# One fixed order for the chunks of eight MoE experts, two norm rows loaded earlier, and the first splits on GpSimd moved

## The chip, the core and the metric

The kernel runs on one core of a Trainium2 chip, as one launch. The core has a matrix engine (TensorE, here PE), a vector engine (VectorE, DVE), a scalar engine (ScalarE, ACT), GpSimd (POOL) and SyncE (SP), which here issues most of the loads. They run side by side and wait for each other by semaphores. The metric is the device time of one execution in microseconds (us); lower is better. All data are float32; a wide product is written as three matmuls of rounded high parts (H) and rests (L) of its factors.

## The reference

The network is two layers of a first block and then one layer of a second block, on 256 positions of width 1024. The change touches the second layer's mixture of experts (MoE), and the norms that stand between the stages. Cut to that:

```python
def swiglu(x, w1, w3, w2):
    return (jax.nn.silu(x @ w1) * (x @ w3)) @ w2

def moe_swiglu(x, router_w, w1, w3, w2):
    logits = (t @ router_w).astype(jnp.float32)      # t: 256 x 1024, 8 experts
    top_v, top_i = lax.top_k(logits, 2)
    gates = jax.nn.softmax(top_v, axis=-1)
    combine = jnp.sum(one_hot(top_i, 8) * gates[..., None], axis=1)
    for e in range(8):
        out = out + combine[:, e:e + 1] * swiglu(t, w1[e], w3[e], w2[e])   # 1024 -> 3584 -> 1024

x = layer_norm(ALPHA * x + mixer(x), ln1_g, ln1_b)
x = layer_norm(ALPHA * x + ffn_or_moe(x), ln2_g, ln2_b)   # dense FFN in layer 0, MoE in layer 1
# block 2: h = rms_norm(x, norm1_g); ... h = rms_norm(x, norm2_g); conv FFN; final norm
```

## The kernel before

**Stages.** Layer 0 (mixer, dense FFN), layer 1 (mixer, MoE), block 2 (mixer, FFN) run one behind the other. The MoE takes from about 660 to 1632 us of the trace.

**Experts and parts.** The router ranks seven of the experts by how many positions they got; expert 0 stands apart. Each rank has slots for a fixed number of positions. Expert 0 and ranks 1, 2, 3 are *wide* (128 slots); ranks 4 to 7 are *narrow* (64 slots). Rank 1 has a narrow part of 64 more slots on the same weights; its chunks are called *heavy* here. If a rank has more positions than slots, a branch (`If`, L1392) runs a second pass; in these runs it isn't taken.

**Chunks.** An expert's 3584 hidden columns are 7 chunks of 512. A chunk needs three loads of 2 MB (`raw`, issued by SP at L155): two up matrices and one down matrix; the down matrix is loaded behind the next chunk's up matrices, since a chunk's down product runs one step later. There are six `raw` buffers, taken in turn. A wide chunk splits its weights (L170 the cast to H on ACT, L172 the subtraction to L on DVE, 12 of each per chunk) and does 48 matmuls up and 24 down in threes (`mm3`, L176 to L178). A narrow part uses the float32 weights as they are, on 64-column halves of the array (`side`, L1247): 64 matmul records up and 16 down, and nothing on ACT and DVE for the weights. So a narrow chunk brings as many bytes as a wide one with less matmul work, and a heavy chunk is a wide and a narrow one's matmuls on one chunk's bytes.

**Gather and scatter.** `gather` (L1144) picks an expert's positions by products with a one-hot matrix `oh` (L1173); the results go to `g` (wide) and `gx` (narrow). `scatter` (L1190) turns `oh`, scales the accumulators `acc` by the gates (L1219, L1220), multiplies by the turned `oh` (L1230) and adds to the stream `xn` (L1231).

**The order of the work.** `moe` (L1357) hands `experts` four groups: (expert 0, rank 4), (rank 2, rank 5), (rank 1 with its second part, rank 7), (rank 3, rank 6). In a group wide and narrow chunks alternate one to one (`turns`; the first group's `lead` begins with two wide ones). A group has one gather and one scatter for all its parts. What else sets the order is the scheduler of the framework, which puts each engine's instructions in a row.

**Norm rows and held splits.** Behind the MoE a layer norm and an RMS norm run for each half (128 positions) of `xn`. The layer norm's g row is loaded into the buffer `rscr`, which the last scatter uses before, ahead of the branch; the b row into `yL` behind the branch (both by ACT's queue, L276). `finish` sets a list `hold` for the first four splits of the next stage: two on GpSimd, issued after the instruction `p`, two on DVE, issued after the last rest of the transposed `xn`. In before, `p` is GpSimd's own power (`rsqrt`, L188) of the second half's norm. `finish` is called at four places that matter: behind layer 0's mixer (about 211 to 224 us), the dense FFN (411 to 424), the MoE (1637 to 1656), and block 2's mixer (1767 to 1781).

## Time and profile before

| | us |
|---|---|
| three runs | 2001.13, 2006.73, 2010.96 |
| median | 2006.73 |
| the profiled execution's own time | 2001.22 |
| its span, first to last instruction | 1999.4 |
| MoE, from the first narrow silu (698.08) to the last (1614.37) | 916.3 |

In the profile, PE is the share of the span in which matmuls run, PEclk the granted clock of TensorE as a part of its full speed, DMA share the mean busy share of the core's 16 DMA engines. "Idle before <-releaser" names what ended an engine's last wait. In a timeline, instructions of one line that follow each other are one row with their count. The PE is busy for 91% of the span, DVE for 60%, ACT for 42%, POOL for 10%; DMA moves 242 GB/s on average. A silu (L1316 wide, L1321 narrow) ends a chunk's up product and is a good clock of the chunks.

### The profile page before, as it was taken

The page shows a single profiled execution, that of the slowest core. Times are in us where ns is not written, and L with a number is a line of the kernel's source. Part 1 is how long each engine was busy: PE and PEld are TensorE (multiplying, and loading weights), DVE is VectorE, ACT ScalarE, POOL GpSimd, SP SyncE. Part 2 cuts the span into 40 slices and gives each one's busy share as a digit, 9 for nine tenths or more (in the row PEclk, how much of TensorE's full clock was granted, in tenths as well). Part 3 has the DMA queues.
Part 4 walks back from the last instruction along what each step waited for, and adds up shares of the span by engine and source line. Part 5 has one row for each costly group of instructions (what it writes and reads, how often), then busy time and mean ns, then how long its engine had stood idle before and what let it go on. Part 6 is the DMA issues. An engine that isn't in the chain of part 4 may idle for free. (4 is left out here: it accounts for less than half of the span.)

```text
span 1999.4 us, 28155 instructions
## 1 busy us (share of the span) xinstructions
PE 1819.5 (91%) x11670; PEld 1408.2 (70%) x11670; DVE 1197.6 (60%) x1717; ACT 842.3 (42%) x1176; POOL 203.4 (10%) x128
## 2 busy tenths in 40 slices
PE   7778899986878999998989999999999868989998
PEld 6666899975656766666666666666666637779997
DVE  6796654578785755355454544344553647667776
ACT  3234344433243545334343443343443525545554
POOL 4251200043323000000000000000000004010000
PEclk9788999998788999999999999999999988799999
DMA  6320536352204799999999777787999944134551
GB/s 241 118 94 23 190 137 243 127 215 85 95 13 169 282 430 418 388 393 355 363 393 384 300 297 305 307 342 315 365 414 390 399 156 164 43 135 171 185 195 64
DMA packets 37574, 484.76 MB, mean 242 GB/s; under 512 B 4544, under 2 KB 5184, under 8 KB 8000
## 3 DMA queue, kind: packets, MB, share of 16 engines
q1 hardware_dynamic: 34992, 475.74, 60.8%
q10 hardware_dynamic: 2448, 7.17, 1.1%
q8 instruction: 93, 1.52, 0.3%
q14 instruction: 41, 0.34, 0.0%
HBM read 481.84 MB, written 1.05 MB: 242 GB/s over the span
## 5 line engine op out<-in xcount | busy, mean ns | idle before, releaser
L172 DVE TENSOR_TENSOR wL<-raw,wH 128x1024 fp32r<-128x1024 f32 (+1 forms) x510 | 616.3, 1229 | 261.9 <-ACT wH L170 250.7
L170 ACT CAST wH<-raw 128x1024 fp32r<-128x1024 f32 x560 | 577.5, 1051 | 401.7 <-PE mm L177 154.0
L1247 PE MATMUL mm<-raw,gx 128*64 128x256 f32 x2240 | 252.3, 381 | 0.0
L1247 PEld LDWEIGHTS mm<-raw,gx 128*64 128x64 f32 x2240 | 156.6, 137 | 85.6 <-issue 10.8
L176 PE MATMUL acc<-wH,hH 128*128 128x512 f32 x408 | 163.8, 416 | 19.8 <-ACT wH L170 19.0
L176 PE MATMUL mm<-wH,g 128*128 128x512 f32 x448 | 177.1, 395 | 0.0
L177 PE MATMUL acc<-wL,hH 128*128 128x512 f32 x408 | 169.7, 416 | 7.2 <-DVE wL L172 7.1
L177 PE MATMUL mm<-wL,g 128*128 128x512 f32 x448 | 175.1, 391 | 0.0
L178 PE MATMUL mm<-wH,g 128*128 128x512 f32 x448 | 174.8, 390 | 0.0
L178 PE MATMUL acc<-wH,hL 128*128 128x512 f32 x408 | 166.8, 410 | 0.0
L172 POOL TENSOR_TENSOR wL<-raw,wH 128x1024 fp32r<-128x1024 f32 x50 | 126.1, 2532 | 135.2 <-ACT wH L170 122.3
L188 POOL TENSOR_TENSOR sm_brs<-sm_brs,half_neg 128x1 f32<-128x1 f32 x8 | 12.1, 1518 | 1207.2 <-DVE sm_brs L186 1207.2
L1247 PE MATMUL acc<-raw,hN 128*64 128x512 f32 x560 | 127.5, 597 | 0.0
L1321 ACT ACTIVATE ff<-mm 128x256 f32<-128x256 f32 x35 | 13.5, 385 | 247.8 <-PE mm L1247 247.8
L176 PEld LDWEIGHTS acc<-wH,hH 128*128 128x128 f32 x408 | 79.1, 197 | 44.4 <-ACT wH L170 22.5
L177 PE MATMUL mm<-b2yL,wH 128*128 128x256 f32 x384 | 109.7, 286 | 0.0
L176 PE MATMUL mm<-b2yH,wH 128*128 128x256 f32 x384 | 109.6, 286 | 0.0
L178 PE MATMUL mm<-b2yH,wL 128*128 128x256 f32 x384 | 109.4, 285 | 0.0
L1322 DVE TENSOR_TENSOR ff<-ff,mm 128x256 f32<-128x256 f32 x35 | 14.7, 421 | 157.2 <-ACT ff L1321 157.2
L177 PEld LDWEIGHTS acc<-wL,hH 128*128 128x128 f32 x408 | 80.2, 197 | 32.3 <-DVE wL L172 14.7
L176 PE MATMUL mm<-y0H,wH 128*128 128x256 f32 x352 | 100.1, 285 | 0.0
L178 PE MATMUL mm<-y0H,wL 128*128 128x256 f32 x352 | 99.8, 284 | 0.0
(518 smaller groups left out, 3263.2 us busy)
## 6 DMA issues: line engine op xcount, KB each, us to landing
raw<-in_moe_dram SPq DMA_DIRECT2D x168, 2048.0 KB, 9.7
raw<-in_ffn_dram SPq DMA_DIRECT2D x33, 2048.0 KB, 7.7
raw<-in_w_in_dram SPq DMA_DIRECT2D x13, 2048.0 KB, 9.2
raw<-in_w_o_dram SPq DMA_DIRECT2D x4, 2048.0 KB, 7.5
row<-in_ln_dram ACTq DMA_DIRECT2D x8, 512.0 KB, 3.6
raw<-in_w_out_dram SPq DMA_DIRECT2D x2, 2048.0 KB, 8.4
raw<-in_w_in_dram SPq DMA_DIRECT2D x3, 1024.0 KB, 5.1
raw<-in_ffn_dram SPq DMA_DIRECT2D x3, 1024.0 KB, 5.2
```

The costliest lines, as they stand in the source:

```text
L170: self.A.copy(H, src)
L172: (eng or self.V).tensor_tensor(L, src, H.bitcast(F32), OP.subtract)
L176: self.T.matmul(out, lhsT=lh, rhs=rh, start=start, stop=False)
L177: self.T.matmul(out, lhsT=lh, rhs=rl, start=False, stop=False)
L178: return self.T.matmul(out, lhsT=ll, rhs=rh, start=False, stop=stop)
L188: return self.G.tensor_tensor(out, out, self.half_neg.to_broadcast([P, n]), OP.pow)
L1247: T.matmul(out[i * 64:i * 64 + 64], lhsT=lhsT, rhs=rhs[:, i * n:i * n + n], start=start, stop=stop)
L1321: A.activation(sn[-1], b[:, 0:256], AF.Silu)
L1322: V.tensor_tensor(sn[-1], sn[-1], b[:, 256:512], OP.mult)
```

## The change

- **One list of steps.** The groups go. Four wide jobs run in the order expert 0, rank 2, rank 1 (heavy), rank 3. A table `FOLLOW` says how many narrow chunks (ranks 4, 5, 6, 7 in this order, 28 in all) follow each wide chunk: 3 in the first job, 4 in the second, 17 in the heavy one, 4 in the last.
- **A gather and a scatter for each job**, and so one for each of nine parts; `gx` has four 64-slot places in turn, and four accumulators are fixed for the whole MoE.
- **Norm rows.** The g and b row of the layer norm behind the MoE go into one tile `gb` of their own, loaded ahead of the branch.
- **Hold.** `layer_norm` and `rms` hand back their last DVE instruction, and `finish` gets that as `p`.

```diff
+FOLLOW = ((0, 1, 0, 1, 0, 1, 0), (1, 0, 1, 0, 1, 0, 1), (2, 3, 2, 3, 2, 3, 2), (1, 0, 1, 0, 1, 0, 1))
...
-        p = self.rsqrt(rs, mv[:, 1:2], 1.0, LN_EPS)
+        self.rsqrt(rs, mv[:, 1:2], 1.0, LN_EPS)
...
-        return p
+        return last
...
-        turns = [(j, c) for c in range(7) for j in range(2)]
...
-        lead = [(0, 0), (0, 1)] + [x for c in range(5) for x in ((1, c), (0, c + 2))] + [(1, 5), (1, 6)]
...
+        jobs = [(part(0), [(0, 0, 0)]), (part(2), [(0, 2, 0)]), (part(1), [(0, 1, 0), (1, 1, P)]), (part(3), [(0, 3, 0)])]
+        narrow = [(j, c) for j in range(4, 8) for c in range(7)]
+        jobs += [(part(r), [(2, r, 0)]) for r in range(4, 8)]
+
+        steps = []
+        for j, follow in enumerate(FOLLOW):
+            for c, n in enumerate(follow):
+                steps += [(j, c)] + narrow[0:n]
+                narrow = narrow[n:]
...
-        g = self.row(a["ln"][1, 2], "rscr")
+        gb = self.xp.tile([P, 2, D], F32, tag="xTL", name="gb", bufs=1)
+        for i in range(2):
+            A.dma_start(gb[:, i], a["ln"][1, 2 + i].partition_broadcast(P))
...
-        b, g2 = self.row(a["ln"][1, 3], "yL"), self.row(a["rows2"][0], "yH")
+        g2 = self.row(a["rows2"][0], "yH")
...
-            self.layer_norm(xn, t, g, b)
+            self.layer_norm(xn, t, gb[:, 0], gb[:, 1])
         for t in range(2):
-            p, *_ = self.rms(xn, t, g2, h)
+            *_, p = self.rms(xn, t, g2, h)
```

**TensorE, in the heavy expert.** `mm3` and `side` write `mm` for up products and `acc` for down products; `gx` holds narrow positions, `hN` a narrow part's hidden columns, `cst` is the identity of a transposition. Before, from a heavy chunk's last up matmul on:

```order
L178 MATMUL mm_9302<-wH_9390,g_8610 128x512
L1247 MATMUL mm_9303<-raw_9297,gx_8611 64x256 x16
L1247 MATMUL acc_9177<-raw_9299,hN_9293 64x512 x8
L182 MATMUL mm_9430<-cst_4_126,ff_9416 128x128 x4
L182 MATMUL mm_9439<-cst_4_126,ff_9419 128x128 x2
L1247 MATMUL mm_9450<-raw_9444,gx_8611 64x256 x16
L1247 MATMUL mm_9450<-raw_9446,gx_8611 64x256 x16
L176 MATMUL acc_8994<-wH_9486,hH_9435 128x512
```

After, from a heavy chunk's last down matmul to the next heavy chunk's first up matmul:

```order
L180 MATMUL acc_5686<-wH_8943,hL_8863 128x512
L1240 MATMUL acc_5687<-raw_8875,hN_8869 64x512 x8
L184 MATMUL mm_8961<-cst_4_126,ff_8910 128x128 x2
L1240 MATMUL mm_8972<-raw_8966,gx 64x256 x16
L1240 MATMUL mm_8972<-raw_8968,gx 64x256 x16
L1240 MATMUL acc_5688<-raw_8970,hN_8964 64x512 x8
L184 MATMUL mm_9016<-cst_4_126,ff_9005 128x128 x2
L1240 MATMUL mm_9027<-raw_9021,gx 64x256 x16
L1240 MATMUL mm_9027<-raw_9023,gx 64x256 x16
L184 MATMUL mm_9071<-cst_4_126,ff_9060 128x128 x2
L1240 MATMUL acc_5688<-raw_9025,hN_9019 64x512 x8
L178 MATMUL mm_9082<-wH_9085,g_8184 128x512
```

Before, one narrow chunk's up product (`mm_9450`) stands between two heavy chunks' work; after, two or three follow each other (here `mm_8972` and `mm_9027`).

**ACT, at the end of the MoE.** Before, from the scaling of the accumulators to the branch:

```order
L1219 ACTIVATE yH_12071<-acc_10823,sm_gc_12050 128x512
L1219 ACTIVATE yH_12071<-acc_10824,sm_gc_12050 128x512
L1219 ACTIVATE rscr_12077<-acc_10961,sm_gc_12060 128x512
L276 DMA row_12110<-in_ln_dram 128x1024
L1386 TENSOR_LOAD idi
L1392 COMPARE_AND_BRANCH
```

After, from the last narrow silu on (four casts and the two `yH` stand between these pieces and the branch):

```order
L1304 ACTIVATE ff_12107<-mm_12074 128x256
L1378 DMA gb<-in_ln_dram 128x1024
L1320 COPY hN_12153<-mm_12150 128x256
L1378 DMA gb<-in_ln_dram 128x1024
L172 CAST wH_12110<-raw_12062 128x1024
```

The load of the norm's first row (`row_12110`) stood behind the last use of its buffer `rscr`, and the second behind the branch; both (`gb`) now stand at the last silu.

**GpSimd, behind the MoE.** `sm_brs` are the powers of the two layer norms, `sm_rms` of the two RMS norms, `wL` the first two held splits. Before:

```order
L188 TENSOR_TENSOR sm_brs_20595<-sm_brs_20595,half_neg 128x1
L188 TENSOR_TENSOR sm_brs_20606<-sm_brs_20606,half_neg 128x1
L188 TENSOR_TENSOR sm_rms_20612<-sm_rms_20612,half_neg 128x1
L188 TENSOR_TENSOR sm_rms_20618<-sm_rms_20618,half_neg 128x1
L172 TENSOR_TENSOR wL_20681<-raw_12104,wH_20680 128x1024
L172 TENSOR_TENSOR wL_20709<-raw_12104,wH_20708 128x1024
```

After:

```order
L190 TENSOR_TENSOR sm_brs_20682<-sm_brs_20682,half_neg 128x1
L174 TENSOR_TENSOR wL_20768<-raw_12216,wH_20767 128x1024
L174 TENSOR_TENSOR wL_20796<-raw_12216,wH_20795 128x1024
L190 TENSOR_TENSOR sm_brs_20693<-sm_brs_20693,half_neg 128x1
L190 TENSOR_TENSOR sm_rms_20699<-sm_rms_20699,half_neg 128x1
L190 TENSOR_TENSOR sm_rms_20705<-sm_rms_20705,half_neg 128x1
```

The two splits have moved ahead, from behind the fourth power to behind the first; the three powers behind them now stand after both. Behind the two earlier stages and block 2's mixer they have moved in the same way, from behind the second half's power to behind the first half's.

## Rows read from the trace of the kernel before

**Rows 1.** Windows, MoE stretches: start:end, length, busy per engine, PEclk, DMA share, GB/s.
```profile
698.00:776.00 78.00, 76.49 (x398) 53.91 (x398) 43.29 (x40) 37.54 (x43) 0.00 (x0) 0.98 1.01 430
776.00:866.00 90.00, 81.39 (x478) 54.50 (x476) 37.77 (x36) 33.49 (x40) 0.00 (x0) 0.98 0.98 396
882.00:1100.00 218.00, 201.69 (x1063) 135.41 (x1063) 104.69 (x109) 86.41 (x101) 0.00 (x0) 0.95 0.95 374
1120.00:1405.00 285.00, 285.00 (x1731) 183.37 (x1728) 127.02 (x141) 106.89 (x139) 0.00 (x0) 1.00 0.79 313
1470.00:1600.00 130.00, 118.45 (x637) 80.95 (x636) 64.58 (x61) 55.98 (x64) 0.00 (x0) 0.97 0.99 402
698.00:1600.00 902.00, 863.04 (x4846) 578.07 (x4845) 444.76 (x479) 377.53 (x465) 0.00 (x0) 0.98 0.91 364
```

**Rows 2.** Timeline, ACT silus: start, duration, engine, line, operation [idle before <-releaser].
```profile
698.08 0.39 ACT L1321 ACTIVATE ff<-mm 128x256 f32<-128x256 f32 x1 [9.28 <-PE mm L1247]
...
1164.33 0.59 ACT L1316 ACTIVATE ff<-mm 128x512 f32<-128x512 f32 x1
...
1203.73 0.59 ACT L1316 ACTIVATE ff<-mm 128x512 f32<-128x512 f32 x1
...
1441.04 0.59 ACT L1316 ACTIVATE ff<-mm 128x512 f32<-128x512 f32 x1
...
1469.20 0.59 ACT L1316 ACTIVATE ff<-mm 128x512 f32<-128x512 f32 x1
...
1598.64 0.59 ACT L1316 ACTIVATE ff<-mm 128x512 f32<-128x512 f32 x1
...
1614.37 0.39 ACT L1321 ACTIVATE ff<-mm 128x256 f32<-128x256 f32 x1 [6.48 <-PE mm L1247]
```

**Rows 3.** Waits from 660 to 1640 us, PE and SPq: total, times, longest.
```profile
PE acc L176 <- ACT wH L170: 19.0, 14, 1.5
...
SPq L155 <- DVE wL L172: 365.4, 60, 24.6
SPq L155 <- PE mm L1247: 319.7, 68, 9.6
```

**Rows 4.** Timeline, PE, one narrow chunk near the end: down, then up.
```profile
1603.02 3.65 PE L1247 MATMUL acc<-raw,hN 128*64 128x512 f32 x16
...
1607.19 7.13 PE L1247 MATMUL mm<-raw,gx 128*64 128x256 f32 x64
```

**Rows 5.** Timeline, PE, one 64-column gather: high halves, then low.
```profile
686.23 1.95 PE L1173 MATMUL mm<-oh,xnH 128*128 128x64 f32 x16
688.01 1.95 PE L1173 MATMUL mm<-oh,xnL 128*128 128x64 f32 x16
```

**Rows 6.** Timeline, PE and DVE, the last down, scatter and add.
```profile
1623.78 3.65 PE L1247 MATMUL acc<-raw,hN 128*64 128x512 f32 x16
...
1627.36 0.50 PE L1230 MATMUL mm<-yH,ohT 128*128 128x512 f32 x1
...
1630.12 2.48 DVE L1231 SCALAR_TENSOR_TENSOR xn<-xn,mm 128x512 f32<-128x512 f32 x4 [1.17 <-PE mm L1230]
```

**Rows 7.** Timeline, POOL and DVE, the norms behind the MoE.
```profile
1650.68 5.10 POOL L172 TENSOR_TENSOR wL<-raw,wH 128x1024 fp32r<-128x1024 f32 x2
...
1643.38 1.41 DVE L270 SCALAR_TENSOR_TENSOR xn<-xn,sm_brs,row 128x512 f32<-128x512 f32 x2 [2.47 <-DMA row<-in_ln_dram]
...
1650.75 5.58 DVE L300 SCALAR_TENSOR_TENSOR h<-xn,sm_rms,row 128x512 f32<-128x512 f32 x2 [0.66 <-POOL sm_rms L188]
```

**Rows 8.** Timeline, DVE, the two norms ahead of the last FFN.
```profile
1769.25 1.42 DVE L300 SCALAR_TENSOR_TENSOR h<-xn,sm_rms,row 128x512 f32<-128x512 f32 x2 [0.67 <-POOL sm_rms L188]
1770.59 0.68 DVE L1459 TENSOR_TENSOR xn<-xn,acc 128x512 f32<-128x512 f32 x1
...
1775.59 5.57 DVE L300 SCALAR_TENSOR_TENSOR h<-xn,sm_rms,row 128x512 f32<-128x512 f32 x2 [0.67 <-POOL sm_rms L188]
```

**Rows 9.** Timeline, DVE, second norm behind the dense FFN.
```profile
416.48 1.28 DVE L268 SCALAR_TENSOR_TENSOR xn<-xn,sm_bmv,row 128x1024 f32<-128x1024 f32 x1
...
418.27 5.49 DVE L270 SCALAR_TENSOR_TENSOR xn<-xn,sm_brs,row 128x512 f32<-128x512 f32 x2
```

More of the change, by code (lines that the diff above doesn't have):

```diff
@@ new lines, in gather @@
+            if (r, slot0) == (0, 0):
+                self.hold = [(self.V, last)] * HOLD0
+            m = 512 // w
+            for k in range(0, KT, m):
+                ks = slice(k, k + m)
+                for src, low in ((xnH, False), (xnL, True)):
+                    b = self.bank()
+                    v = b.rearrange("p (k s) -> p k s", k=m)
+                    for kk in range(m):
+                        for t in range(2):
+                            T.matmul(v[:, kk], lhsT=src[:, t, (k + kk) * P:(k + kk + 1) * P], rhs=oh[:, t, 0:w],
+                                     start=t == 0, stop=t == 1)
+                    if not low:
+                        A.copy(x[0][:, ks], v)
+                    elif narrow:
+                        V.tensor_tensor(x[0][:, ks], x[0][:, ks], v, OP.add)
+                    else:
+                        V.tensor_copy(x[1][:, ks], v)
@@ L1189, in scatter @@
+            got.append((narrow, r, oh, x))
+        return got
+    def scatter(self, got, cmp_, xacc, scale):
         V, A, T = self.V, self.A, self.T
@@ L1264, in down, with gather, last @@
                             self.mm3(acc[n], h[0][:, j], h[1][:, j], H[:, 0, ns], L[:, 0, ns], *ends)
-        steps = [(g, j, c) for g in groups for j, c in g[2]]
-        pend, rest, late, into = None, None, [], None
-        parts_of = lambda g: sorted(p for w, parts in g[0] for p in parts)
-        def gather(g):
-            nonlocal into, late
-            now = [p for p in parts_of(g) if len(g) < 4 or p in g[3]]
-            late = [p for p in parts_of(g) if p not in now]
-            into = self.gather(xnH, xnL, pl, now)
-        def put_of(g):
-            return self.scatter(state["oh"], cmp_, [p[0:2] for p in parts_of(g)], lambda: state["acc"], xacc, g[1])
-        gather(groups[0])
-        for n, (g, j, c) in enumerate(steps):
-            w, parts = g[0][j]
-            new = n == 0 or steps[n - 1][0] is not g
-            if between and g is groups[1]:
-                between()
-                between = None
-            if new:
-                oh, gH, gL, gx = into
-            if late and late[0] in parts:
-                self.gather(xnH, xnL, pl, late, into)
-                late = []
+        got = {}
+        def gather(n):
+            j, c = steps[n]
+            if c == 0:
+                got[j] = self.gather(xnH, xnL, pl, jobs[j][1])
+        def last():
+            nonlocal scale
+            (j, c), hs = pend
+            rd, put = self.load(jobs[j][0](c, 2)), None
+            if c == 6:
+                put = self.scatter(got[j], cmp_, xacc, scale)
+                scale = 1.0
+                next(put)
+            return c, hs, rd, put
+        gather(0)
+        pend, rest = None, None
+        for n, (j, c) in enumerate(steps):
+            w = jobs[j][0]
+            if between and n == len(steps) // 4:
+                between()
             raws = [self.load(w(c, i)) for i in range(2)]
@@ L1323, in experts @@
-            if n + 1 < len(steps) and steps[n + 1][0] is not g:
-                gather(steps[n + 1][0])
+                g, u = (b[0][:, 0:256], b[0][:, 256:512]) if narrow else b
+                s = s[:, 0:256] if narrow else s
+                A.activation(s, g, AF.Silu)
+                V.tensor_tensor(s, s, u, OP.mult)
+                ss.append((narrow, s))
+            if n + 1 < len(steps):
+                gather(n + 1)
             if pend:
-                down(c0, hs, rd)
-            hs = {}
+                down(*lo)
@@ L1346, in experts @@
                 rest = put
-            if new:
-                state.update(acc={}, oh=oh)
-            pend = ((g, j, c), hs)
-        (g0, j0, c0), hs = pend
-        rd = self.load(g0[0][j0][0](c0, 2))
-        put = put_of(g0)
-        next(put)
-        down(c0, hs, rd)
+            pend = ((j, c), hs)
+        *lo, put = last()
+        list(rest or ())
+        down(*lo)
         list(put)
@@ L1377, in part @@
             return ap
[L1379 to L1382 removed]
+        b = [self.bank("acc") for i in range(4)]
+        self.accs = {0: b[0:2], 1: b[2:3], 2: b[3:4]}
+        self.gx = self.xp.tile([P, KT, 4, 64], F32, tag="xTL", name="gx", bufs=1)
```

181 lines of the change are left out of this document (71 added, 110 removed).

## Prediction

> **What bounds the kernel now.** I read the windows of the MoE stage first [rows 1]. Over 698 to 1600 us PE is busy for 863 of 902 us, and DMA for 0.91 at 364 GB/s, so both are near their limit on average; the stretches show that they take turns. From 1120 to 1405 us, the group with the heavy chunks, PE is busy all the time and DMA for only 0.79. From 1470 to 1600 us and from 776 to 866 us DMA is at 0.98 to 0.99, with 402 and 396 GB/s, and PE has gaps. What one stretch leaves unused the other lacks, and with six buffers only two chunks can be carried over. The silus turn this into times for a chunk [rows 2]. A heavy chunk with one narrow chunk takes 1203.73 - 1164.33 = 39.40 us. A wide with a narrow one where PE sets the pace takes 1469.20 - 1441.04 = 28.16 us. The difference, 11.24 us, is a narrow part, and so a wide chunk is 28.16 - 11.24 = 16.92 us. Where DMA sets the pace, four pairs take 1598.64 - 1469.20 = 129.44 us, 32.36 for a pair and 5.39 us for each of its six loads. The waits agree [rows 3]: PE's largest wait there is 19.0 us, for casts in the down products, and SP's loads wait for buffers, 365.4 us for DVE's last read and 319.7 us for narrow matmuls.
>
> **The change part by part.**
>
> **The order of chunks.** It takes nothing away; it lays the narrow chunks, which cost 3 x 5.39 = 16.2 us of DMA and 11.24 us of PE, beside the heavy ones, which cost 28.16 us of PE and the same DMA. That 11.24 us is right for a lone narrow chunk too: its down row of 3.65 us and its up row of 7.13 us make 10.8 us without the transposes [rows 4]. Both kernels have the same work done at 698.08 us (two wide chunks and a narrow one), and both end with a narrow chunk, so I count from the first narrow silu to the last, 916.3 us before [rows 2]. In between lie 53 chunks or 159 loads: 5 wide and 2 narrow in the first job, 7 and 4 in the second, 7 heavy and 17 narrow in the third, 7 and 4 in the last.
>
> PE's side: 84.6 + 22.5 = 107; 118.4 + 45.0 = 163; 197.1 + 191.1 = 388; and 163 us. To this come gathers and scatters. A 64-column gather is 32 matmuls in about 3.6 us (two rows of 16 that begin 1.78 us apart) [rows 5], hardly less than a wider one, since each matmul needs its own weights; seven parts inside the window make 25 us, where three shared gathers made 11: the change adds 14 us. A part's scatter is eight matmuls of some 0.27 us (16 for two parts from 1627.36 us to about 1631.8) and under 1 us of transposes [rows 6], together 3 us; there are as many as before. By job that gives about 111, 177, 413 and 167 us, 868 in all. The adds on DVE (four in 2.48 us [rows 6]) become 32 instead of 16, some 10 us spread over a stage where DVE is busy for half the time [rows 1], and I cost them at nothing; were all of them on the path, they would cost 10.
>
> DMA's side at 5.39 us for a load: 21 loads 113, 33 loads 178, 72 loads 388, 33 loads 178 us. The larger of both, job by job: 113 + 178 + 413 + 178 = 882 us, **34 less than 916**. Jobs two and four are still DMA's, by little, and job three is PE's. The ends: if the six buffers even out the jobs too, PE's 868 remains, 48 less. If loads go at the pace of 882 to 1100 us (374 GB/s, so 2.097 MB in 5.61 us [rows 1]), the jobs are 118, 185, 413 and 185 us, 901 in all, 15 less. I stay with 5.39, which is from the stretch where DMA is nearest to full.
>
> **The end of the MoE.** The last narrow down product (3.65 us) now runs mostly behind the wide scatter and no longer beside the scaling of the wide accumulators, and the narrow scatter has its own four adds behind it. Before, the adds end at 1630.12 + 2.48 = 1632.6 us [rows 6]; the new row of PE's order gives an end 1 to 2 us later.
>
> **Norm rows.** Before, the first half's layer norm waits 2.47 us for a row [rows 7]. Loaded at the last silu, the rows are there 20 us ahead, so the wait goes; what is late next is GpSimd's power, about 0.3 us earlier, so 2.1 us are to be had.
>
> **The hold.** The order shows that the splits are not held: an edge to a DVE instruction leaves no wait on GpSimd, and the splits stand behind the first half's power, earlier than before. Beside two of them (5.10 us) a DVE norm pair that takes 1.41 us takes 5.5 to 5.6 [rows 7, 8]. So the 4.1 us are not gone but move from the second half to the first, and the second half's power now stands behind the splits on GpSimd. The Trainium skill ("SBUF — State Buffer", section "SBUF: two separate sides") explains such rows: DVE and GpSimd share a port pair, and whoever has it keeps it for a whole instruction. By that rule a real hold would free the second half at each place, and by it these splits block the first half as they blocked the second; the rows agree, 5.58 against 1.41 us.
>
> What that is worth differs by place. Behind the MoE the first pair ends 1.9 us later than before (the row's 2.1 us are inside that) and the second 4.1 us sooner: -2.2. Ahead of the last FFN the residual add at 1770.59 us stands behind the first pair on DVE [rows 8], so it begins at about 1774.7, the second half's whole chain follows it, and the pair that ended at 1781.16 ends within 0.5 us of that; if DVE gets in ahead of the first split there, 1.6 us are gained: -0.8. Behind the dense FFN the casts for the splits come late enough for the first pair to pass; the splits then block the long operation at 416.48 us [rows 9] by about 2 us, and the last pair, 5.49 us before, is free again: -1.9. Behind layer 0's mixer gain and delay cancel. With the tail's +1.5 this is **-3 us**, and 6 to either side bounds it: the second-half block gone in two places without a price, or the first-half block unreturned in two.
>
> **Sum.** -34 - 3 = -37. The profiled execution has a span of 1999.4 us and a time of 2001.2, and would go to about 1964; it lies 5.5 us under the median of 2006.7. I put the difference on the median: 2006.7 - 37 = **1970 us**.
>
> **The rivals.**
>
> *DMA is the bound throughout, at the pace it has on average.* If 364 GB/s, the mean of 698 to 1600 us [rows 1], were what the path sustains and not what the order allowed, 159 loads would take 159 x 5.76 = 916 us whatever the order, and the time would be about 2004. Against it are 430, 402 and 396 GB/s in three stretches; for it are the 374 GB/s at a share of 0.95. The Trainium skill ("DMA: Bandwidth & Descriptors", section "Specifications") puts one core's share of memory bandwidth at about 358 GB/s. By that figure the loads alone would take an estimated 931 us and the kernel would be slower by 12 or so; the 402 GB/s over 130 us speak against it.
>
> *The runs of narrow chunks starve: slower.* In the heavy job two or three narrow chunks follow each other. Each lacks 16.2 - 11.24 = 4.9 us of loads, 17 x 4.9 = 84 us in all, and only a lead built during the heavy chunks (28.16 us of PE, 16.2 of DMA, so 12 us each) pays for it. It can be built only as far as buffers are free, and the current chunk holds three of six; SP has waited up to 24.6 us for one [rows 3]. If no lead came over, job three would take 413 + 84 = 497 us, the MoE 966, and the kernel 2006.7 + 50 - 3 = 2054. It decides between faster and slower where DMA idles for 34/84 of those 12 us, 5 us, in every heavy step. Against it: from 1120 to 1405 us, with one narrow chunk behind each heavy one, PE never waited [rows 1], and a free set of three buffers is 16 us of loads, about what a run of three lacks (14.8).
>
> *The splits are held after all, or block more.* A hold that works would take 4.1 us off four second halves, 16 us, and end at about 1957 with the rest as forecast; first-half blocks with nothing given back cost 16 us and would give 1989. Neither turns the sign.
>
> **How the numbers follow.** Forecast (15 to 48 us from the order): 0.78, the held or blocking splits included. DMA at its mean: 0.12. Starved runs: 0.10, of which a light form (some idle, still within 10 us) is 0.02. The range goes from the PE-bound case with the norms' best, -48 - 6, so about 1952, to the slow loads with the norms' worst, -15 + 6, so about 1998; the two rivals at 2004 and 2054 lie beyond it, and I leave them out as the two in ten. A change of 0.5%, 10 us, is about what a measurement of this kernel can tell from none. The forecast's cases nearly all lie below 1996.7: faster 0.79; same 0.13; slower 0.08.
>
> **What would show it.** In the profile after, the last narrow silu should stand some 34 us earlier counted from the first. In the heavy job PE should be busy nearly all the time, with a DMA share over 0.9 instead of 0.79; gaps ahead of the second and third narrow chunk of a run would show starved runs. In jobs two and four pairs of loads should take 5.2 to 5.6 us each; 5.8 with DMA full would show the DMA rival. Gather rows should come to 3.6 us for each part. The first norm pair at the end of the MoE should take 5.5 us and the second 1.4, with no wait for a row. I would be wrong if PE idles in the heavy job, or if the wide chunks that now follow each other, with DVE at 12 splits a chunk, wait for DVE.

## The result, and the profile after

| | before | after |
|---|---|---|
| median, us | 2003.8 (6 runs, 2000.39 to 2010.96) | 2022.67 (6 runs, 2016.94 to 2029.25) |
| ratio to before, 95% interval | | 1.009 (1.0064 to 1.0115) |
| the profiled execution: time, span | 2001.22, 1999.4 | 2020.36, 2018.6 |
| MoE, first to last narrow silu | 916.3 | 949.0 |
| from the start to the first narrow silu | 698.1 | 692.1 |
| from the last narrow silu to the end | 385.0 | 377.6 |

The change makes the kernel about 19 us slower; 37 us faster was forecast. The MoE lost 32.7 us, and the stages around it gained 13.5. First the four jobs, cut at the last silu of each, and the whole MoE of the kernel after, as windows (start:end, length, busy per engine in the order PE, PEld, DVE, ACT, POOL, granted clock, DMA share, GB/s; [rows 1] answer to them):

```profile
692.09:799.44 107.35, 104.57 (x526) 78.16 (x527) 72.74 (x66) 64.25 (x71) 0.00 (x0) 0.98 0.99 406
799.44:1000.27 200.83, 186.43 (x934) 135.51 (x933) 120.28 (x126) 97.92 (x112) 0.00 (x0) 0.96 0.91 346
1000.27:1454.63 454.36, 440.73 (x2732) 270.71 (x2733) 148.26 (x177) 119.44 (x164) 0.00 (x0) 0.98 0.84 336
1454.63:1641.04 186.41, 171.97 (x888) 122.75 (x888) 106.88 (x103) 91.92 (x105) 0.00 (x0) 0.98 0.94 365
692.09:1641.04 948.95, 903.70 (x5076) 607.12 (x5076) 448.16 (x472) 373.53 (x449) 0.00 (x0) 0.98 0.89 351
```

The jobs take 107, 201, 454 and 186 us where 113, 178, 413 and 178 were forecast. TensorE is idle for 45.3 us, and DMA has room in three of the four jobs. The waits of the same stretch (total us, times, longest), PE's and those of SP's load queue; [rows 3] answer to them:

```profile
PE mm L178 <- ACT wH L172: 17.6, 11, 2.3
PE mm L184 <- DVE ff L1305: 11.3, 12, 0.9
PE acc L178 <- ACT wH L172: 7.0, 5, 1.4
PE mm L179 <- DVE wL L174: 5.3, 10, 0.8
PE acc L179 <- DVE wL L174: 3.6, 7, 0.5
...
SPq L157 <- DVE wL L174: 361.2, 66, 9.9
SPq L157 <- PE mm L1240: 315.8, 68, 11.4
```

These add to 44.8 of the 45.3 us. The rest is one wait of 0.3 for the adds of a scatter. None is a wait for a load, and in the whole stretch ACT never waited for one either: the loads wait for buffers. The silus of the second job (as in [rows 2]) show where a chunk loses time:

```profile
853.05 0.59 ACT L1304 ACTIVATE ff<-mm 128x512 f32<-128x512 f32 x1
...
890.02 0.38 ACT L1304 ACTIVATE ff<-mm 128x256 f32<-128x256 f32 x1 [6.72 <-PE mm L1240]
907.44 0.59 ACT L1304 ACTIVATE ff<-mm 128x512 f32<-128x512 f32 x1
```

Two wide chunks and a narrow one take 907.44 - 853.05 = 54.4 us. By the forecast's prices of TensorE's work they should take 2 x 16.92 + 11.24 = 45.1.

The norms went much as forecast. Behind the MoE (POOL and DVE), behind the dense FFN and ahead of the last FFN (DVE), with [rows 7 to 9] as their counterparts:

```profile
1669.40 5.08 POOL L174 TENSOR_TENSOR wL<-raw,wH 128x1024 fp32r<-128x1024 f32 x2
1669.46 5.56 DVE L272 SCALAR_TENSOR_TENSOR xn<-xn,sm_brs,gb 128x512 f32<-128x512 f32 x2 [0.31 <-POOL sm_brs L190]
...
1680.98 1.41 DVE L302 SCALAR_TENSOR_TENSOR h<-xn,sm_rms,row 128x512 f32<-128x512 f32 x2 [0.66 <-POOL sm_rms L190]
```

```profile
418.26 3.29 DVE L270 SCALAR_TENSOR_TENSOR xn<-xn,sm_bmv,row 128x1024 f32<-128x1024 f32 x1
422.07 1.40 DVE L272 SCALAR_TENSOR_TENSOR xn<-xn,sm_brs,row 128x512 f32<-128x512 f32 x2
...
1790.60 3.56 DVE L302 SCALAR_TENSOR_TENSOR h<-xn,sm_rms,row 128x512 f32<-128x512 f32 x2 [0.66 <-POOL sm_rms L190]
...
1799.07 1.42 DVE L302 SCALAR_TENSOR_TENSOR h<-xn,sm_rms,row 128x512 f32<-128x512 f32 x2 [0.67 <-POOL sm_rms L190]
```

The first pair now takes 5.56 us beside the splits and the last one 1.41; the wait for the row is gone.

**What a stall looks like.** Before, in a pair of the last group: the ACT rows of a timeline, then the PE rows of the same place.

```profile
1484.92 0.39 ACT L1321 ACTIVATE ff<-mm 128x256 f32<-128x256 f32 x1 [6.48 <-PE mm L1247]
1486.34 0.37 ACT L1342 COPY hN<-mm 128x256 f32<-128x256 f32 x1 [1.04 <-PE mm L182]
1486.61 4.84 ACT L170 CAST wH<-raw 128x1024 fp32r<-128x1024 f32 x5
...
1485.81 0.44 PE L182 MATMUL mm<-cst,ff 128*128 128x128 f32 x2 [0.94 <-DVE ff L1322]
1487.71 0.50 PE L176 MATMUL acc<-wH,hH 128*128 128x512 f32 x1 [1.46 <-ACT wH L170]
1488.97 0.50 PE L177 MATMUL acc<-wL,hH 128*128 128x512 f32 x1 [0.53 <-DVE wL L172]
```

ACT idles for 6.48 us, because its next instruction is the narrow silu, which waits for the narrow up product. Behind the silu stand the copy to `hN` and only then the casts of the wide chunk's down matrix. TensorE, done with the up product, waits for silu, cast and subtraction in turn: 0.94, 1.46 and 0.53 us. In the groups without heavy chunks most pairs have this: 14 times between the first and the last narrow silu PE waits for `ff`, 0.94 us each. The heavy group has none.

After, the same happens in the heavy job, where a wide chunk's first casts stand behind the run of narrow chunks (ACT, then PE):

```profile
1187.03 0.39 ACT L1304 ACTIVATE ff<-mm 128x256 f32<-128x256 f32 x1 [6.64 <-PE mm L1240]
1192.27 0.37 ACT L1320 COPY hN<-mm 128x256 f32<-128x256 f32 x1 [4.85 <-PE acc L1240]
1192.54 3.89 ACT L172 CAST wH<-raw 128x1024 fp32r<-128x1024 f32 x4
...
1187.92 0.44 PE L184 MATMUL mm<-cst,ff 128*128 128x128 f32 x2 [0.94 <-DVE ff L1305]
...
1193.64 0.50 PE L178 MATMUL mm<-wH,g 128*128 128x512 f32 x1 [1.16 <-ACT wH L172]
...
1197.39 0.63 PE L179 MATMUL mm<-wL,g 128*128 128x512 f32 x1
...
1198.88 0.39 PE L180 MATMUL mm<-wH,g 128*128 128x512 f32 x1
```

The casts had not been waiting for their data. By the order of the loads, their matrix was issued at 1165.56 us and landed 10.5 us later, so it lay in memory for 16 us before the first cast at 1192.54.

Behind the stall a matmul takes 0.63 us instead of 0.39. The windows on that place show why (columns as above, the third from the right is the granted clock):

```profile
1195.30:1198.20 2.90, 2.90 (x8) 2.26 (x7) 2.90 (x3) 2.12 (x3) 0.00 (x0) 0.50 0.99 424
1199.00:1203.00 4.00, 4.00 (x24) 2.90 (x24) 2.95 (x3) 3.06 (x4) 0.00 (x0) 1.00 0.52 221
```

The granted clock is 0.50, the lower of its two levels (1.2 GHz), for 2.9 us behind the idling of 0.94 and 1.16 us, and full again behind that. So this stall costs its idle time and some slower matmuls after it. Not every stall does: behind the idling of 1.62 and 0.76 us that ends at 1510.44 us, the matmuls after that one take 0.39 to 0.40 us, and the granted clock from 1509 to 1514 us is 1.00.

The kernel after has 18 such places: one in the first job, six in the second (three at a narrow chunk behind a wide one, as in before, and three where one wide chunk follows another and its first casts come too late), five in the heavy job as just shown, and six in the last, again three of each kind.

### The profile page after: what moved, and what is told of

Read it like the earlier page. It is cut to its first block, busy times and chain, and to the rows that moved or that the text cites. A ratio compares the mean times of both kernels' runs of the same rounds, so it can differ in the third digit from the quotient of the medians.

```text
span 2018.6 us, 28423 instructions
## 1 busy us (share of the span) xinstructions
PE 1837.6 (91%) x11798; PEld 1422.3 (70%) x11798; DVE 1206.5 (60%) x1715; ACT 837.9 (42%) x1158; POOL 200.1 (10%) x128
## 4 chain that ended last, share of the span: by engine, by line
issue 52%; PE 31%; DVE 13%; ACT 1%; POOL 1%; POOLq 0%; DVEq 0%; ACTq 0%
PE mm L178 5%; PE mm L179 5%; PE mm L180 5%; PE acc L178 3%; PE acc L179 3%; PE acc L180 3%; DVE cv L854 3%; PE mm L184 1%; DVE t L604 1%; DVE wL L174 1%; DVE xn L272 1%; DVE cq L513 1%; PE mm L969 1%; PE mm L1652 0%; PE mm L945 0%
## 5 line engine op out<-in xcount | busy, mean ns | idle before, releaser
L1240 PE MATMUL mm<-raw,gx 128*64 128x256 f32 x2240 | 258.3, 382 | 0.0
L1305 DVE TENSOR_TENSOR ff<-ff,mm 128x256 f32<-128x256 f32 (+1 forms) x63 | 34.0, 539 | 300.4 <-ACT ff L1304 214.2
L178 PE MATMUL mm<-wH,g 128*128 128x512 f32 x448 | 181.8, 406 | 17.6 <-ACT wH L172 17.6
L179 PE MATMUL mm<-wL,g 128*128 128x512 f32 x448 | 180.9, 404 | 5.3 <-DVE wL L174 5.3
L180 PE MATMUL mm<-wH,g 128*128 128x512 f32 x448 | 178.7, 399 | 0.0
L1304 ACT ACTIVATE ff<-mm 128x256 f32<-128x256 f32 (+1 forms) x63 | 30.0, 476 | 259.9 <-PE mm L1240 259.9
L1240 PE MATMUL acc<-raw,hN 128*64 128x512 f32 x560 | 133.8, 604 | 0.0
L178 PEld LDWEIGHTS mm<-wH,g 128*128 128x128 f32 x448 | 87.0, 194 | 43.3 <-ACT wH L172 22.7
L179 PEld LDWEIGHTS mm<-wL,g 128*128 128x128 f32 x448 | 86.9, 194 | 27.2 <-DVE wL L174 9.7
```

What stands on the lines that cost most here:

```text
L178: self.T.matmul(out, lhsT=lh, rhs=rh, start=start, stop=False)
L179: self.T.matmul(out, lhsT=lh, rhs=rl, start=False, stop=False)
L180: return self.T.matmul(out, lhsT=ll, rhs=rh, start=False, stop=stop)
L1240: T.matmul(out[i * 64:i * 64 + 64], lhsT=lhsT, rhs=rhs[:, i * n:i * n + n], start=start, stop=stop)
L1304: A.activation(s, g, AF.Silu)
L1305: V.tensor_tensor(s, s, u, OP.mult)
```

## The experiments

The expectations call theories by letters and say what each means. Theory A is that TensorE is short of loads, by bytes or by buffers. Theory C, formed after the first eight runs, is the one above: TensorE waits for casts that stand too far back in ACT's row.

### The parts: the order alone, the norms alone, the old hold

Run e1_even keeps the one list of steps with its own gather and scatter for each job, but lays the narrow chunks one behind each wide one, as before:

```diff
-FOLLOW = ((0, 1, 0, 1, 0, 1, 0), (1, 0, 1, 0, 1, 0, 1), (2, 3, 2, 3, 2, 3, 2), (1, 0, 1, 0, 1, 0, 1))
+FOLLOW = ((0, 1, 1, 1, 1, 1, 2), (1,) * 7, (1,) * 7, (1,) * 7)
```

> The kernel after, with the table of narrow chunks set to one behind each wide chunk, as the kernel before had it; the nine gathers, the fixed accumulators, the norm rows and the splits stay as after. Theory A, that the order itself lengthens the stage (loads wait for one of six buffers while DMA has nothing to do, in the runs of narrow chunks and between two wide chunks): first to last narrow silu falls from 949 to 916 + 14 (four more gathers) = 930 us or a little less, and the kernel from 2022.7 to about 2003. Theory B, that the extra gathers, the scatters and the fixed accumulators cost the time: it stays at 949 and 2022.

Measured: 2011.05 us, ratio 1.005 (1.0029 to 1.0071); the MoE from the first to the last narrow silu 929.1 us. That is theory A's 930 for the MoE, though not its 2003 for the kernel, and the run can't say why the order costs time. The gathers and scatters of single parts cost 929.1 - 916.3 = 12.8 us (14 forecast), and the new order of chunks another 949.0 - 929.1 = 19.9, where it should have saved about 48.

Run e2_norms has the groups of before with `gb` and the new hold alone:

```diff
-        p = self.rsqrt(rs, mv[:, 1:2], 1.0, LN_EPS)
+        self.rsqrt(rs, mv[:, 1:2], 1.0, LN_EPS)
...
-        g = self.row(a["ln"][1, 2], "rscr")
+        gb = self.xp.tile([P, 2, D], F32, tag="xTL", name="gb", bufs=1)
```

> The kernel before with the other two parts alone: the norm rows loaded early into their own tile, and the norms' last DVE operation given to the list of held splits; chunks, gathers and scatters as before. From the forecast's own steps: 2.1 us behind the dense FFN, 2.2 behind the MoE, 1 to 2 ahead of the last FFN, 0 behind the first mixer, so 5 to 6 us under before, 1998. If the profile of after shows more of this part's doing (its stages outside the MoE are 13.4 us shorter than before's, 4.7 of them at the four norms), 12 to 15 us under before, about 1990.

Measured: 1993.56 us, ratio 0.9961 (0.9935 to 0.9987), the MoE 917.3 us. The norm part with all that comes with it gains some 8 us, between the two figures expected. The loss of the change is all in the MoE.

Run e3_oldhold is the kernel after with `p` again GpSimd's power:

```diff
-        self.rsqrt(rs, mv[:, 1:2], 1.0, LN_EPS)
+        p = self.rsqrt(rs, mv[:, 1:2], 1.0, LN_EPS)
...
-        return last
+        return p
```

> The kernel after with GpSimd's power given to the held splits again, as before; the order of the chunks and the early norm rows stay. If the hold's move brought the gain outside the MoE: 2022.7 plus 4 (only the four norms) to 12 us (the two mixers too), 2027 to 2035. If it brought nothing: 2022 to 2024.

Measured: 2034.09 us, ratio 1.0143 (1.0096 to 1.019). It lies in the expected range and points the same way as e2_norms, but its size can't be read as the hold's price: its first stage, which the hold has no part in, ends 9 us later (the first norm's power at 221.96 instead of 213.01 us). The norms themselves can be read. From the first power to the last pair's end, those behind the dense FFN and ahead of the last FFN take 12.72 and 12.49 us with the old hold, as in before, so the new one is worth about 2 us at each. Behind the MoE they take 14.50 us with the old hold and 14.47 with the new one: there the early rows are the whole gain.

### Bytes, buffers and runs

Run e4_halfbytes loads for narrow chunks only the first half of each matrix and reads it twice; the matmuls stay as they are.

```diff
-            raws = [self.load(w(c, i)) for i in range(2)]
+            raws = [self.load(w(c, i)[:, :2048], 2048) if j > 3 else self.load(w(c, i)) for i in range(2)]
...
-                            side(b[0][:, i * 256:i * 256 + 256], x[0][:, k], raw[:, k], *ends)
+                            side(b[0][:, i * 256:i * 256 + 256], x[0][:, k], raw[:, k % 4 if j > 3 else k], *ends)
```

> The kernel after, but each load of a narrow chunk brings half its bytes, and the matmuls read that half twice: the same work on every engine, 84 half loads. Its result is not the reference's. Theory A in the form that narrow runs starve: the heavy job (last narrow silu of one job to that of the next, 454 us in after) falls to the 413 us of PE's work, and the second and fourth job (200.8 and 186.4) to 167 to 177. If what the second and fourth job lose is DVE's splits of a wide chunk behind a wide chunk: these two stay above 185, and only the heavy job falls.

Measured: 1946.33 us in one run, the MoE 871.0 us. Its four jobs, as windows:

```profile
692.73:795.44 102.71, 102.71 (x524) 77.18 (x525) 73.09 (x66) 64.49 (x71) 0.00 (x0) 1.00 0.87 352
795.44:970.25 174.81, 174.81 (x931) 129.87 (x930) 126.41 (x130) 104.08 (x115) 0.00 (x0) 1.00 0.84 330
970.25:1398.14 427.89, 426.95 (x2737) 267.48 (x2738) 149.59 (x177) 123.47 (x164) 0.00 (x0) 0.99 0.64 232
1398.14:1563.68 165.54, 165.54 (x889) 120.90 (x890) 109.23 (x103) 94.46 (x104) 0.00 (x0) 1.00 0.86 335
```

TensorE never stops, and needs 871 us for the work of the new order; the forecast's sum for it was 868. I took this for theory A at first: fewer bytes, no stalls. But a second thing had changed with the bytes. The scheduler lays the rows of the engines ahead of the run, and with the shorter loads it laid ACT's differently (ACT at the same heavy step as the stall above):

```profile
1135.37 0.38 ACT L1305 ACTIVATE ff<-mm 128x256 f32<-128x256 f32 x1 [6.43 <-PE mm L1240]
1139.49 3.89 ACT L172 CAST wH<-raw 128x1024 fp32r<-128x1024 f32 x4 [3.74 <-DMA raw<-in_moe_dram]
...
1152.19 0.38 ACT L1305 ACTIVATE ff<-mm 128x256 f32<-128x256 f32 x1 [6.64 <-PE mm L1240]
```

The four casts now stand ahead of the last narrow chunk's silu and begin 13 us before it; in the kernel after they began 5.5 us behind it. So the run couldn't tell bytes from the place of the casts.

Four runs went after theory A's buffers and the lengths of runs. In e5_halftiles three of the six buffers are split into six halves, each with a load of 1 MB, so that room comes free in smaller pieces:

```diff
+            raw = self.mp.tile([P, 2048], F32, tag="raw", name=f"raw{self.chunk}_{h}", bufs=2 * MORE)
+            self.nc.sync.dma_start(raw, ap[:, h * 2048:h * 2048 + 2048])
```

> The kernel after, but three of the six weight buffers of the MoE are six of half the size, and a load into them is two of 1 MB: the same memory, bytes and order, and a half is free as soon as its own matmuls and splits are done. Theory A, that the order leaves DMA idle because no buffer is free during a heavy chunk (loads in after are issued 9 to 13 us apart there, at 5.4 us each) and between two wide chunks: the idle 8 us for each heavy chunk about halves, first to last narrow silu falls from 949 to 905 to 930 us and the kernel to 1980 to 2004. Theory B, that DMA delivers no more than its 345 to 350 GB/s in this order, whatever is free: within 5 us of 2022.7.

Measured: 2037.49 us, ratio 1.0189 (1.0155 to 1.0224), the MoE 960.8 us: worse, and in neither theory's range. Its trace has 20 stalls of the kind above, where the kernel after has 18.

In e6_five (the kernel after) and e7_five_before (the kernel before) there are five buffers instead of six:

```diff
-MORE = 3
+MORE = 2
```

> The kernel after with five weight buffers in the MoE, not six. Theory A: each heavy chunk's lead falls by one load, 5.4 us, so the heavy job (454) takes 25 to 40 us more and the jobs with two wide chunks in a row 10 to 20 more each: first to last narrow silu 995 to 1030. Theory B: within 10 of 949.

> The kernel before with five weight buffers in the MoE. Theory A: an order with one narrow chunk behind each wide one asks for less lead; its heavy group, where DMA had 21% to spare, loses little (under 10 us), the others some: first to last narrow silu from 916 to 930 to 960, less of a loss than after's. Theory B: within 10 of 916.

Measured, in one run each: 2031.84 us (the kernel after) and 2000.14 us (the kernel before). The MoE takes 946.9 us with five buffers and 949.0 with six in the kernel after, 919.7 and 916.3 in the kernel before. A buffer less to load ahead into changes nothing that matters, in either order. That is against theory A; both lie where theory B put them. The 9 us that e6_five takes over the kernel after as a whole are not in the MoE.

In e9_two each heavy chunk is followed by two narrow ones and the rest goes to the other jobs:

```diff
+FOLLOW = ((0, 1, 0, 1, 1, 0, 1), (1, 0, 1, 1, 0, 1, 1), (2, 2, 2, 2, 2, 2, 2), (1, 0, 1, 1, 0, 1, 1))
```

> The kernel after with two narrow chunks behind each heavy one (14), 4 in the first job and 5 in the second and fourth. Theory A, by the periods of after (a heavy chunk with two narrow ones 55 to 57 us, two wide and one narrow 54.5, a wide and a narrow one 32.4): between the even order's 929 and after's 949, about 937, and the kernel near 2013. If only runs of three hurt: 915 and 1990. If the extra gathers were the cause: 949 and 2022.

Measured: 2023.05 us, ratio 1.012 (1.0078 to 1.0162), the MoE 955.0 us. Runs of three aren't the trouble, and theory A's 937 is missed. The nearest figure is that of the extra gathers, but e1_even, with the same gathers, had shown that they don't explain 949. Its trace has 19 stalls of the kind above: 12 with a wait for `ff`, seven more with one for a wide chunk's first cast alone.

### The casts

Run e10_casts changes the kernel after in one thing: where a narrow chunk follows a wide one, the four casts of the wide chunk's down matrix stand ahead of the narrow silu on ACT, and at the end of a run of two or three narrow chunks the first four casts of the next wide chunk stand ahead of the last silu of the run. Loads, buffers and TensorE's work are the same.

```diff
+                if wide(n - 1):
+                    rd = lo[2].rearrange("p (f d) -> p f d", d=D)
+                    made = [self.split(rd[:, i:i + 1], (1, D)) for i in range(4)]
+                    mark = self.cast
+                elif wide(n + 1):
...
-                A.activation(s, g, AF.Silu)
+                with self.tc.issue_after(mark.ins) if mark else nullcontext():
+                    A.activation(s, g, AF.Silu)
```

> The kernel after, same chunks, bytes and buffers; the four casts of a wide chunk's down matrix are written ahead of the following narrow chunk's silu, and at the end of a run of narrow chunks the first four casts of the next wide chunk ahead of the last narrow chunk's silu, with an order edge on ACT each time. Theory C, that the loads are in long before they are used (five buffers changed nothing; a matrix issued at 1165.6 us was first read at 1192.5) and TensorE waits for casts that stand in ACT's queue behind a narrow chunk's silu and copy, which themselves wait for TensorE: the waits for ACT's wH (25 us in 16 pieces, and the low clock behind each) go, first to last narrow silu falls from 949 to 885 to 915 us and the kernel to 1960 to 1990. Theory A, that data come late: a silu forced behind a cast that waits for data makes it no better, 949 or more and 2022 or more.

Run e11_even_casts is the same in e1_even's order (`FOLLOW` as there).

> The same early casts with one narrow chunk behind each wide one, as before. Theory C: from 929 to 880 to 905 us, the kernel from 2011 to 1965 to 1990; both orders then come near TensorE's own sum of 868 to 871 us, and what is left between them is small. Theory A: 929 or more.

Measured: e10_casts 1984.07 us, ratio 0.9925 (0.9899 to 0.995), the MoE 907.9 us; e11_even_casts 1948.55 us, ratio 0.9746 (0.9687 to 0.9804), the MoE 877.2 us. The casts alone take 41 us off the new order and 52 off the even one, with every byte still loaded. Theory C holds, though it asked too little of the even order (1965 to 1990) and the two orders are still 31 us apart, not close. Its bookkeeping closes on what e10_casts left. Its largest PE waits, and the window of two wide chunks and a narrow one:

```profile
PE mm L178 <- ACT wH L172: 8.3, 6, 1.6
PE mm L184 <- DVE ff L1320: 6.8, 1, 6.8
PE mm L179 <- DVE wL L174: 4.6, 6, 0.8
```

```profile
853.55:903.22 49.67, 47.29 (x236) 34.61 (x235) 32.21 (x30) 27.10 (x31) 0.00 (x0) 0.97 0.95 371
```

The six waits for `wH` are the six places where a wide chunk follows a wide one, which the edit leaves alone. Each costs 49.67 - 45.1 = 4.6 us, six of them 27, and with the one wait of 6.8 that is 34 of the 37 us between e10_casts and e4_halfbytes. The wait of 6.8 is of the same kind: at the end of a narrow expert in the heavy job, a silu stands on ACT behind the scaling of that expert's accumulator, which waits 10.41 us for TensorE, and behind the four casts.

But for that one place the heavy job of e10_casts has its casts in time, with all its bytes, and so it tells the two apart, as e4_halfbytes could not:

```profile
992.84:1427.63 434.79, 426.88 (x2691) 265.12 (x2691) 147.77 (x177) 119.09 (x164) 0.00 (x0) 0.98 0.86 347
```

It takes 434.8 us, where the kernel after took 454.4 and e4_halfbytes 427.9. What is left over e4_halfbytes is that one wait; TensorE's busy time is the same 427 us, and no wait of TensorE there is for a load.

Run e12_groups_casts tries the same on the groups and shared gathers of before, with the norm part of the change:

```diff
+            made, mark = None, None
+            if not main and 0 in hs:
+                rv = rd.rearrange("p (f d) -> p f d", d=D)
+                made = [self.split(rv[:, i:i + 1], (1, D)) for i in range(4)]
+                mark = self.cast
```

> The order of before (chunks group by group, the gathers shared between the two chunks of a pair) with the norm part of the change and with the early casts of the run before. Theory C (TensorE waits for casts queued behind the narrow silus, whatever the order of the chunks): the stretch from the first to the last narrow silu falls from 917 us to about 864 us, which is the 877 us of the even order with early casts less the 13 us that its additional gathers cost; the kernel about 1936 us. Rival (DMA binds in the pairs of before, where its share was already .98 to .99): the stretch stays at 905 to 917 us and the kernel at 1980 to 1993 us.

Measured: 1938.6 us, ratio 0.9707 (0.9667 to 0.9746), the MoE 862.3 us, where theory C had 1936 and 864. In its last group, ACT and PE at a place like the first stall above:

```profile
1402.04 1.05 ACT L170 CAST wH<-raw 128x1024 fp32r<-128x1024 f32 x1
1408.62 0.39 ACT L1327 ACTIVATE ff<-mm 128x256 f32<-128x256 f32 x1 [5.54 <-PE mm L1247]
...
1407.76 0.82 PE L1247 MATMUL mm<-raw,gx 128*64 128x256 f32 x6
1408.51 0.50 PE L176 MATMUL acc<-wH,hH 128*128 128x512 f32 x1
```

A cast (the last of the four) is done in what was idle time, and the down product (its first matmul is in the last row) follows the up product with no gap. Its windows of the second and the last group, and of the whole MoE:

```profile
881.36:1058.00 176.64, 175.15 (x986) 122.36 (x987) 98.35 (x100) 85.17 (x105) 0.00 (x0) 1.00 1.01 430
...
1392.90:1554.13 161.23, 158.65 (x899) 108.82 (x898) 85.76 (x81) 74.48 (x87) 0.00 (x0) 0.99 1.00 421
691.88:1554.13 862.25, 858.17 (x4945) 577.85 (x4946) 449.09 (x484) 379.60 (x470) 0.00 (x0) 1.00 0.93 386
```

This is the fastest of all the kernels run, 3% under before. TensorE is busy for 858 of 862 us, and DMA gives 421 to 430 GB/s in the pairs, where before it gave 402 and 396 at shares of 0.99 and 0.98.

Run e13_even_casts_five asks whether loads are next: e11_even_casts with five buffers (the edit of e6_five).

> The even order with early casts, with five load buffers in place of six. Where TensorE is busy throughout, theory C expects nothing of the sixth buffer as long as loads still land before their casts: first to last narrow silu 877 us, within 3 us. If DMA has become the bound in this kernel (its share is 1.00 in three of the four jobs), a buffer less takes from what it can run ahead in the job with the heavy steps: the stretch grows by 5 to 15 us.

Measured, in one run: 1958.88 us, the MoE 883.5 us, 6.3 more than with six. ACT's waits for loads:

```profile
ACT wH L172 <- DMA raw<-in_moe_dram: 37.7, 14, 9.8
```

With six buffers that was one wait of 1.1 us. So ACT now meets loads that are late, and the 6.3 us lie in the range of the other expectation. But TensorE doesn't wait for them: its idle time between the two silus is 5.5 us with five buffers and with six, and it has no wait for a cast that the run with six buffers hasn't. The 6.3 us are slower matmuls in one stretch, where the two kernels do the same work (1058.39 to 1115.57 us here; the granted clock is 1.00 there with six buffers):

```profile
1062.00:1072.00 10.00, 10.00 (x34) 8.58 (x34) 4.84 (x6) 2.66 (x3) 0.00 (x0) 0.51 1.00 424
```

TensorE was busy throughout and had not idled ahead of it either (its last wait before ended at 882.85 us). Why the clock fell there the run doesn't show, and nothing in it says that the sixth buffer begins to count.

## Why the prediction was wrong

| kernel | stalls | MoE, us | the same order with casts in time | for one stall |
|---|---|---|---|---|
| before | 14 | 916.3 | 862.3 (e12_groups_casts) | 3.9 |
| e1_even | 12 | 929.1 | 877.2 (e11_even_casts) | 4.3 |
| after | 18 | 949.0 | 871.0 (e4_halfbytes, half the narrow bytes) | 4.3 |

A stall is counted where PE waits for `ff` or, without that, for the first cast of a wide chunk. The count goes with the time in the other runs too: 14 stalls in e2_norms and e7_five_before (917.3 and 919.7 us), 18 in e3_oldhold and e6_five (945.8 and 946.9), 19 in e9_two (955.0), 20 in e5_halftiles (960.8).

**The step that failed is the reading of the bound,** "where DMA sets the pace, four pairs take ... 5.39 us for each of its six loads". A pair took 32.36 us not because six loads take that long. It took TensorE's 28.16 and a stall of 4.2: 2.9 us of idling (0.94 + 1.46 + 0.53) and some 1.3 of slower matmuls. The 4.2 us were shared out over six loads and became a price of DMA. In e12_groups_casts the pairs of the last group take 28.16 us each, so six loads go through at 4.69 each. Two rows spoke against the reading. In [rows 3] SP's loads had waited 685 us for buffers that subtractions and matmuls held, and PE's largest wait was for a cast; a queue that waits for its consumers isn't what they wait for. I named both and took them to agree with it. The DMA share of 0.98 to 0.99 [rows 1] persuaded me, and it isn't a rate: at 0.99 DMA moved 402 GB/s and at 1.00 to 1.01 up to 430. The Trainium skill ("Perfetto Trace Analysis", section "Identifying the Most-Contended Engine") says the occupancy of the 16 DMA engines misleads and asks for the achieved bandwidth instead; these rows agree. The Trainium skill, on the same page (section "Engine Utilization"), puts the practical ceiling of a core that is active alone at about 120% of 358 GB/s, which makes an estimated 430; e12_groups_casts reached that and passed it in no window shown here.

**"The larger of both, job by job" therefore compared TensorE's sum with a pace that was no limit.** TensorE's side itself was right in sum, 868 against 871 us in e4_halfbytes. By job it was 111, 177, 413 and 167 against 103, 175, 428 and 166: 8 us too much in the first and 15 too little in the heavy job, and that the sum came out is in part luck. What the sum lacked was a price for each place where ACT's row makes TensorE wait. The new order has four more of these than the old one. By job, after less e4_halfbytes is 4.6, 26.0, 26.5 and 20.9 us for 1, 6, 5 and 6 stalls. By the table, 24 of the +32.7 us of the MoE are stalls (78.0 us against 54.0: four more, and each a little dearer), and the other 8.7 are the work without them (871.0 against 862.3), the gathers and scatters included. The -34 was the price of a wait for loads that TensorE didn't have. The time was there to be won, 54 us of stalls in before, but by the row of ACT and not by the order of the chunks. Idle time (45.3 us) and slower matmuls (TensorE's busy time 903.7 instead of 870.0, so 33.7) make up the 78 us of stalls in the kernel after.

**The gathers** were right: 14 forecast, 12.8 between e1_even and before (12 stalls against 14), 14.9 between e11_even_casts and e12_groups_casts, which have next to none. **The adds on DVE**, costed at nothing, stay there: in e4_halfbytes TensorE waits 0.9 us for them.

**The rival "the runs of narrow chunks starve"** had the sign and the place, the heavy job (454 us, 413 forecast, 497 by the rival), and the signs it named came true: TensorE idles there, and DMA is at 0.84 and so idle for 73 us, 10 for each heavy step, twice the 5 at which it was to decide. Its mechanism is refuted. The gaps stand at the transposes behind the run and at the next wide chunk's first matmuls, not ahead of the second and third narrow chunk; and a buffer less makes no difference. DMA's idling was no sign of hunger at all: in the same job of e10_casts, where TensorE has one wait left, DMA is at 0.86, since TensorE's 427 us of work there take longer than the loads (72 at the 4.69 us of e12_groups_casts would be an estimated 338). **The rival "DMA at its mean pace"** is refuted by 386 GB/s over the whole MoE of e12_groups_casts, against the 364 it took as the limit.

**"If the wide chunks that now follow each other ... wait for DVE"** was named as a way to be wrong. It is six of the 18 stalls, but ACT comes first there: 1.62 us for the cast, then 0.76 for the subtraction (PE, in the last job of the kernel after):

```profile
1509.19 0.50 PE L178 MATMUL mm<-wH,g 128*128 128x512 f32 x1 [1.62 <-ACT wH L172]
1510.44 0.50 PE L179 MATMUL mm<-wL,g 128*128 128x512 f32 x1 [0.76 <-DVE wL L174]
```

**The norms** were right in their mechanism. From the last narrow silu to the norm's first instruction the end of the MoE is 1.58 us longer (+1.5 forecast), by luck: the last adds end 4.1 us later, not 1 to 2, and DVE then waits 1.87 us for the branch instead of 4.39; from the first power to the last pair's end the norms behind the MoE take 14.47 instead of 16.66 us, so -2.2 as forecast; behind the dense FFN 10.65 instead of 12.72, -2.1 (-1.9); ahead of the last FFN 10.47 instead of 12.49, -2.0 (-0.8, or -1.6 if DVE gets in ahead of the first split, which the 3.56 us suggest it did); behind the first mixer nothing. The splits moved ahead and were not held, as the order had shown. Two gains were not forecast: the mixer behind the dense FFN is 4.8 us shorter beyond its norm (216.6 to 209.7 us with it), and block 2's mixer 4.7 us (112.3 to 107.6). Over all the kernels run these two stages take from 209.0 to 216.6 and from 104.7 to 115.8 us, also where an edit touches only the MoE's chunks (e6_five, which has one buffer less than the kernel after, takes 214.6 and 114.0). So these stages move by some 5 us either way without an edit of their own, and neither gain, nor all of e2_norms' 8 us, can be put down to the norms. Between e6_five and the kernel after, the mixer behind the dense FFN differs in TensorE's clock: TensorE idles for 42 us in both and is busy for 172.8 us instead of 167.5, with a granted clock of 0.50 in 8 us (from 581.54) where the kernel after has 1.00. What moves the clock, and what the other differences are, no run settles.

**Open:** the new order with all its casts in time and all its bytes was not run. In e10_casts the heavy job, which has both but for one place, has no wait of TensorE for a load; the six places where a wide chunk follows a wide one were never mended. That they are of the same kind is argued from their waits and their price. Less its 34 us of waits and what stands behind them, e10_casts would come to an estimated 874 us (907.9 - 34).

## What to carry to other kernels

When a matmul stage seems to be bound by transfers, ask who waits for whom: if the load queue waits for buffers and no consumer waits for data, the transfers aren't the bound, however full they look. On an engine that serves both the next step's preparation and this step's result, put the preparation that is ready ahead of the instruction that must wait; here four casts ahead of a silu were worth 54 us, more than any order of the chunks. Price an order of steps by the places where such a row makes TensorE wait, with the slower clock that may follow. And before a difference of a few us is put down to an edit, compare TensorE's busy time and its granted clock over the same work.

## What the runs showed of the hardware

- In the kernel after, TensorE's granted clock was 0.50 for 2.9 us (from 1195.30 us) behind idling of 0.94 and 1.16 us, and a matmul of 512 columns took 0.63 us instead of 0.39. Behind idling of 1.62 and 0.76 us (to 1510.44 us) the clock stayed at 1.00, and such matmuls took 0.39 to 0.40. In e13_even_casts_five the clock was 0.51 for 10 us with TensorE busy before and throughout. Over the MoE of the kernel after, TensorE was busy for 33.7 us more than in e4_halfbytes, beside 45.3 us of idling.
- A stretch at a DMA share of 0.99 moved 402 GB/s and others at 1.00 to 1.01 moved 421 to 430: the share did not show how much was left.
- ACT keeps its row: in the kernel after it idled for 6.64 us ahead of the silu at 1187.03 us, while the matrix of the casts behind it had landed at 1176.06. The Trainium skill ("PSUM — Partial Sum Buffer", section "Engine vs sequencer instructions") calls its queue strictly first in, first out, and the rows agree.
